# First attention of a two-layer encoder: q, k and v split by token and transposed by DMA, rope tables that carry the norm weights, O divided from PSUM

## The chip, the cores and the metric

The kernel runs on one core of a Trainium2 chip. The core has TensorE (PE, with its weight loads PEld), VectorE (DVE), ScalarE (ACT), GpSimd (POOL) and SyncE (SP), which here issues most of the DMAs. The metric is the device time of one execution in microseconds; the time of a kernel is the median of its runs. A profile shows one execution, with every instruction's start and duration.

## The reference

Two layers of an encoder trunk on one sequence of 1024 tokens of width 1024. Layer 0 mixes tokens by multi-head latent attention, layer 1 by dilated window attention, and each ends with a squared-ReLU MLP. The change is in layer 0's mixer:

```python
proj = h @ w_in
q_lat, kv_lat = proj[..., :384], proj[..., 384:640]
k_rope = rope(proj[..., 640:], pos)
q = (rms_norm(q_lat, g_qa) @ w_qb).reshape(B, S, 16, 96)
kv = (rms_norm(kv_lat, g_kva) @ w_kvb).reshape(B, S, 16, 128)
q = concat([q[..., :64], rope(q[..., 64:], pos)])
k = concat([kv[..., :64], broadcast(k_rope)])
v = kv[..., 64:]
q, k = rms_norm(q, g_q), rms_norm(k, g_k)
o = dense_attention(q, k, v, 96 ** -0.5)      # softmax over all 1024 keys, 16 heads
y = o.reshape(B, S, 1024) @ w_o
```

Products that need more than 16 bits of precision are made from two f16 parts, a high and a low one: high x high, high x low, low x high.

## The kernel before, in words

**Heads stage** (in `mla`, pool `psB`, lines 882 to 953). For each half of the heads (`hf`, 8 heads) and each tile of 128 tokens (`t`): TensorE makes q (two batches of 4 heads, 384 columns) and kv (two of 512 columns) in four PSUM banks (`mm3`, lines 522 to 524). ACT squares them (L905, L907), DVE sums the squares (L909, L910) and `rstd` makes 1/rms. DVE multiplies q and k by it into the f32 tile `st` (L921, L924), ACT copies v (L920), POOL writes the rotary part of k (L926) and rotates q (`rope`, L599 to L604, six instructions a batch). SP stores `st`, 256 f32 a token and head, to the DRAM tensor `qkv` (L933). The norm weights of q and k are multiplied together into one column `gq`. In the second half, the loads, preparations and maxima of heads 0 and 1 stand between the steps. This stage is put in order by the language's scheduler, except where an instruction is pinned.

**Preparation of a head** (`prep_load`, `prep`). Two loads bring the head's rows of `qkv` back (L813). TensorE turns q and k, four f32 transposes at a time (L826). ACT writes the high half from PSUM, scaled by `gq` or 64 (L156), and DVE the low half (L158). v is split the same way from SBUF into a tile with a column of ones (L161). A 97th row of k is a constant, that of q is minus the row's maximum, so that the score matmul subtracts it.

**Maxima** (`rowmax`, `rowstore`). For each of 8 tiles of queries and each half of the keys one matmul of high parts (L859) and a DVE reduction (L861). Then a small reduction (L867), a transpose to a row (L868), an ACT copy (L870), and two DMA steps through DRAM put it into q's row 96 (L871, L872).

**Attention** (`attention`). 128 slots, n = 8 x head + key tile. In a slot PE does two score banks of three 512-column matmuls (L1139 to L1141), then the AV products of slot n - 3 (L1178 to L1182): p is stationary, v moves, and for each of 8 query tiles the columns hold p_high x (v_high, 1, v_low) and p_low x (v_high, 1). ACT makes the exponentials (L1150), ACT or DVE the high half (L1154, L1152), POOL, or DVE in one slot of 8, the low half (L1161). At a head's end ACT and DVE copy the two AV banks out (`evict`), DVE takes reciprocals (L1201), and POOL adds the two v parts and divides (L1204 to L1208). For each pair of heads O is turned (L1217) and split (`spread`). The lists `todo`, `mid`, `late` and `end` say what else a slot does and where; `pin_from` keeps every engine in the order in which the code emits. Every fourth slot `ada_step` loads 512 KB of weights and adds 1024 columns on DVE (L261). PSUM has three score banks, two AV banks and three banks ("t") for everything else: maxima, transposes, sums.

After attention follow the output projection, layer 0's MLP and layer 1.

Of the kernel before, what the change touches and what calls it, by code (L numbers as in the profile page):

```python
# [20 lines left out]
P = 128  # L21
# [20 lines left out]
class K:  # L42
# [83 lines left out]
    def rstd(self, ms, n, name, up=False):  # L126

        nc = self.nc
        y = self.sm(name + "y", n)
# [72 lines left out]
    def const_loads(self):  # L202
# [16 lines left out]
        for r, src in ((5, "mla_g_q"), (6, "mla_g_k")):  # L219
            nc.gpsimd.dma_start(out=self.rows2[r : r + 1, 0:QK], in_=a[src])  # L220

# [383 lines left out]

    def w_in(self, d):
# [14 lines left out]
    def mla(self, xs, ada0, xs1, mods, tail):  # L621
# [177 lines left out]
        if half:  # L799
            most = self.M("most", [P, 16])  # L800
            nc.gpsimd.memset(most, 0.0)
            lnp = self.M("lnp", [P, 1])
            nc.gpsimd.memset(lnp, 10.0 * math.log(2.0))
        qkv = self.DR([H, S, 256], "qkv")
# [3 lines left out]
        ld, rd = (self.DR([H, S], x) for x in ("lrow", "rrow"))  # L808
# [6 lines left out]
        def prep(h, part, pt):  # L815
# [13 lines left out]
            if half:  # L829
                self.parts(hi, lo, pt[0:QK, :], gq if n == "q" else 64.0, check=False)  # L830
                if part < 2:
                    v4, ts = hd["v"][:, 0:1032].rearrange("p (t e) -> p t e", e=129), slice(4 * i, 4 * i + 4)
                    self.parts(v4[:, ts, 0:64], v4[:, ts, 65:129], hd["raw"][i][:, :, 192:256])
                    if i == 1:
                        nc.gpsimd.memset(v4[:, :, 64:65], 1.0)
                return
# [25 lines left out]

        def rowstore(h, ps):

            if half:
                nm = self.sm("nm", 8)
                nc.vector.tensor_reduce(nm, maxes.pop(h).rearrange("p (j b) -> p j b", b=2), op=ALU.max, axis=AX.X, negate=True)  # L867
                nc.tensor.transpose(ps[0:8, 0:P], nm, self.ident)  # L868
                mr = self.T("mr", (8, P), F16)
                nc.scalar.activation(mr, ps[0:8, 0:P], AF.Copy, scale=1.0 / 128)  # L870
                nc.sync.dma_start(out=md[h].rearrange("(t p) -> t p", p=P), in_=mr)  # L871
                nc.sync.dma_start(out=heads[h]["qh"][QK : QK + 1, :], in_=md[h : h + 1, :])  # L872
                return
# [8 lines left out]
        with tc.tile_pool(name="psB", bufs=8, space=PSUM, reuse_waits="tile") as psp:  # L882
            B = lambda name: psp.tile([P, 512], F32, tag="b", name=self.nm(name))
            raw = None
            for hf in range(2):
                w = hw[hf]
                for t in range(NT):
# [12 lines left out]
                    st = [self.G("st", (P, 4, 256), F32) for b in range(2)]  # L900
# [12 lines left out]
                    r = self.rstd(ms, 16, "hr", half)  # L913
                    if half:
                        y4 = self.sm("y4", 16)
                        nc.gpsimd.tensor_tensor(y4, r, r, op=ALU.mult)
                        nc.gpsimd.tensor_tensor(y4, y4, y4, op=ALU.mult)
                        nc.gpsimd.tensor_tensor(most, most, y4, op=ALU.add)
                    for b in range(2):
                        nc.scalar.activation(st[b][:, :, 192:256], kv4[b][:, :, 64:128], AF.Copy, scale=2.0 ** -7 if half else 1.0)  # L920
# [3 lines left out]
                        nc.vector.tensor_tensor(st[b][:, :, 96:160], kv4[b][:, :, 0:64],  # L924
                                                rk.broadcast_to([P, 4, 64]), op=ALU.mult)
                        nc.gpsimd.tensor_tensor(st[b][:, :, 160:192], rk.broadcast_to([P, 4, 32]),  # L926
                                                kr[:, t : t + 1, :].broadcast_to([P, 4, 32]), op=ALU.mult)
                    for b in range(2):
                        qr = st[b][:, :, 64:96]
                        self.rope(nc.gpsimd, qr, qr, *(self.cs[k][:, t : t + 1, :].broadcast_to([P, 4, 16])  # L930
                                                       for k in ("cos", "sin")), 4, "qr")
                        h0 = hf * 8 + b * 4
                        nc.sync.dma_start(out=qkv[h0 : h0 + 4, ts, :].rearrange("h t e -> t h e"), in_=st[b])  # L933
                    if hf == 0:
# [6 lines left out]
                        raw = heads_load(1, t) if t < 5 else None  # L941
                    else:
# [13 lines left out]
        if half:  # L956
            self.nseen += 1
            s_ = self.seen[:, self.nseen - 1 : self.nseen]
            nc.vector.tensor_reduce(s_, most, op=ALU.add, axis=AX.X)
            nc.vector.tensor_scalar(s_, s_, 2.0 ** 41, None, op0=ALU.mult)  # L960
            return self.attention(heads, gq, lnp, prep_load, prep, rowmax, rowstore, tail), None
# [151 lines left out]
    def attention(self, heads, gq, lnp, prep_load, prep, rowmax, rowstore, tail):  # L1113
# [5 lines left out]
        OP, U = {}, {}  # L1119
        with tc.tile_pool(name="psC", bufs=2, space=PSUM, reuse_waits="tile") as psp:  # L1120
# [3 lines left out]
            todo, mid, late, end = {}, {}, {}, {}  # L1124
# [21 lines left out]
            def weights(n, ps):  # L1146

                p, q = self.G("p", dt=F32), self.G("pp", (P, 2, 1024), F16)
                for b in range(2):
                    nc.scalar.activation(p[:, b * 512 : (b + 1) * 512], ps[b], AF.Exp, scale=1.0 / self.ss, bias=lnp)  # L1150
                if n % 8 in (0, 5):
                    nc.vector.tensor_copy(q[:, 0], p)  # L1152
                else:
                    nc.scalar.activation(q[:, 0], p, AF.Copy)  # L1154
                ps_p[n] = p, q

            def low(n):

                p, q = ps_p[n]
                eng = nc.vector if n % 8 == 3 or n > N - 4 else nc.gpsimd  # L1160
# [3 lines left out]
            def av(n):  # L1164
# [4 lines left out]
                v = heads[h]["v"][:, kt * 129 : kt * 129 + 129]  # L1169
                q = ps_p.pop(n)  # L1170
                mm = nc.tensor.matmul
                for b, ps in enumerate(ps_u[h]):
                    for i in range(4):
                        c = slice((4 * b + i) * P, (4 * b + i + 1) * P)
                        o = ps[:, 129 * i : 129 * i + (129 if i < 3 else 65)]
                        st = kt == 0 and i == 0
                        if i < 3:
                            mm(o, q[:, 0, c], v, start=st, stop=False)  # L1178
                        else:
                            mm(o, q[:, 0, c], v[:, 0:65], start=False, stop=False)  # L1180
# [1599 lines left out]
```

## Time and profile before

| what | value |
|---|---|
| median of 3 runs | 3082.59 us (3081.91 to 3087.77) |
| the profiled execution | 3090.18 us, its span 3088.3 us |
| busy: PE, DVE, ACT, POOL | 93%, 76%, 54%, 30% of the span |
| mean DMA rate | 161 GB/s |

The busy shares are of the whole span, in which stages with different limits follow each other. A row of a group of instructions gives line, engine, operation, the tiles out and in, shapes, count, then busy us and the mean ns of one, then the idle time of the engine ahead of it and what ended that. A row of the timeline gives start and duration in us.

### The profile page before, as it was taken

How to read it: one execution, taken by the hardware profiler on the slowest of the kernel's cores; microseconds unless marked ns; L12 is line 12 of the kernel's file. 1: busy time of each engine (PE TensorE's matmuls, PEld its weight loads, DVE VectorE, ACT ScalarE, POOL GpSimd, SP SyncE). 2: the span in 40 equal slices, each digit the busy share in tenths (PEclk: the TensorE clock that was granted, in tenths of full speed). 3: DMA queues.
4: the chain of work that ended last, by engine and by line, in shares of the span. 5: the costliest groups of instructions: out<-in, count | busy, mean ns of one | idle time of the engine just before them, and what ended most of it. 6: DMA issues, size and time to landing. Idle time of an engine off the chain costs nothing. (4 is left out here: it accounts for less than half of the span.)

```text
span 3088.3 us, 53769 instructions
## 1 busy us (share of the span) xinstructions
PE 2876.5 (93%) x19636; PEld 1712.4 (55%) x19636; DVE 2340.4 (76%) x5049; ACT 1666.9 (54%) x3443; POOL 933.3 (30%) x1521
## 2 busy tenths in 40 slices
PE   5998888889999999999999999997998999999998
PEld 4744555554444444444448878886876444444443
DVE  4688878865898895679867777776887589779665
ACT  3546777672545543443127787776665265545431
POOL 6376777660021100000113343443554002110010
PEclk7999999999999999999999999999998999999999
DMA  5253221141565579755734766675656556447653
GB/s 201 73 195 113 76 83 60 66 144 68 196 239 177 211 239 300 216 195 182 249 117 120 162 136 141 144 166 113 137 124 153 148 191 214 161 152 275 231 196 96
DMA packets 485053, 498.73 MB, mean 161 GB/s; under 512 B 191781, under 2 KB 373330, under 8 KB 484778
## 3 DMA queue, kind: packets, MB, share of 16 engines
q1 hardware_dynamic: 449162, 396.56, 44.0%
q0 software_dynamic: 25184, 87.12, 7.6%
q10 hardware_dynamic: 10432, 11.54, 1.5%
q8 instruction: 155, 2.54, 0.3%
q14 instruction: 120, 0.98, 0.1%
HBM read 329.90 MB, written 125.12 MB: 147 GB/s over the span
## 5 line engine op out<-in xcount | busy, mean ns | idle before, releaser
L522 PE MATMUL psm<-hf,wf 128*128 128x512 f16 x896 | 340.6, 380 | 6.3 <-ACT wf L156 6.3
L523 PE MATMUL psm<-d,d 128*128 128x512 f16 x896 | 340.5, 380 | 4.7 <-DVE d L161 4.7
L524 PE MATMUL psm<-hf,wf 128*128 128x512 f16 x896 | 334.9, 380 | 7.6 <-DVE wf L161 7.6
L524 PE MATMUL psm<-d,d 128*128 128x512 f16 x896 | 340.5, 380 | 0.0
L523 PE MATMUL psm<-hf,wf 128*128 128x512 f16 x896 | 340.3, 380 | 0.0
L522 PE MATMUL psm<-d,d 128*128 128x512 f16 x896 | 334.7, 380 | 0.3 <-ACT d L156 0.3
L522 PE MATMUL psproj<-wqk,hTp 128*128 128x256 f16 x1024 | 284.4, 278 | 0.0
L523 PE MATMUL psproj<-wqk,hTp 128*128 128x256 f16 x1024 | 283.6, 277 | 0.0
L524 PE MATMUL psproj<-wqk,hTp 128*128 128x256 f16 x1024 | 283.2, 277 | 0.0
L1161 POOL TENSOR_TENSOR pp<-p,pp 128x1024 f16<-128x1024 f32 x109 | 244.0, 2247 | 103.2 <-ACT pp L1154 81.4
L156 ACT ACTIVATE d<-ufr 128x1024 f16<-128x1024 f32 x112 | 117.8, 1052 | 205.3 <-PE psm L524 168.2
L161 DVE SCALAR_TENSOR_TENSOR d<-ufr,d 128x1024 f16<-128x1024 f32 x112 | 136.5, 1219 | 77.9 <-ACT d L156 77.7
L861 DVE TENSOR_REDUCE mx<-pmx 128x1 f32<-128x512 f32 x256 | 163.0, 678 | 23.5 <-PE pmx L859 23.4
L1150 ACT ACTIVATE p<-pss,lnp 128x512 f32<-128x512 f32 x256 | 163.0, 679 | 22.3 <-PE pss L1141 21.2
L2259 ACT ACTIVATE pd<-pd,dnb 128x192 f32<-128x192 f32 (+2 forms) x384 | 167.3, 437 | 4.2 <-POOL y L2187 2.2
L524 PEld LDWEIGHTS <-wf 128*128 128x128 f16 x896 | 87.8, 98 | 118.3 <-DVE wf L161 14.0
L522 PEld LDWEIGHTS <-wf 128*128 128x128 f16 x896 | 87.7, 98 | 114.5 <-ACT wf L156 12.2
L524 PEld LDWEIGHTS <-d 128*128 128x128 f16 x896 | 87.7, 98 | 110.6 <-issue 5.7
L522 PEld LDWEIGHTS <-d 128*128 128x128 f16 x896 | 87.9, 98 | 106.3 <-issue 1.9
L523 PEld LDWEIGHTS <-d 128*128 128x128 f16 x896 | 87.8, 98 | 106.0 <-issue 1.7
L2297 POOL TENSOR_TENSOR ph<-pd,ph 128x512 f16<-128x512 f32 (+1 forms) x121 | 113.2, 942 | 108.2 <-ACT ph L2296 108.0
L523 PEld LDWEIGHTS <-wf 128*128 128x128 f16 x896 | 87.8, 98 | 104.5 <-issue 1.0
(442 smaller groups left out, 8229.3 us busy)
## 6 DMA issues: line engine op xcount, KB each, us to landing
ufr<-uf SPq DMA_DIRECT2D x112, 512.0 KB
adaw<-in_ada_w SPq DMA_DIRECT2D x96, 512.0 KB
w2r<-in_mlp_w SPq DMA_DIRECT2D x96, 512.0 KB
w1r<-in_mlp_w SPq DMA_DIRECT2D x64, 512.0 KB
wqkr<-in_dil_w_in SPq DMA_DIRECT2D x96, 256.0 KB
wvr<-in_dil_w_in SPq DMA_DIRECT2D x34, 512.0 KB
qkv<-st SPq DMA_DIRECT2D x32, 512.0 KB
hraw<-qkv SPq DMA_DIRECT2D x32, 512.0 KB
```

Of the source, the lines that this page charges most:

```text
L156: nc.scalar.activation(hi, src, AF.Copy, scale=scale)
L161: return nc.vector.scalar_tensor_tensor(lo, src, scale, hi, op0=ALU.mult, op1=ALU.subtract, accum_out=self.seen[:, self.nseen - 1 : self.n ...
L522: mm(out, lh, rh, start=first, stop=False)
L523: mm(out, lh, rl, start=False, stop=False)
L524: mm(out, ll, rh, start=False, stop=last)
L861: nc.vector.tensor_reduce(maxes[h][:, 2 * j + b : 2 * j + b + 1], ps, op=ALU.max, axis=AX.X)
L1150: nc.scalar.activation(p[:, b * 512 : (b + 1) * 512], ps[b], AF.Exp, scale=1.0 / self.ss, bias=lnp)
L1161: eng.tensor_tensor(q[:, 1], p, q[:, 0], op=ALU.subtract)
L2259: nc.scalar.activation(p[:, e, lo:hi], p[:, e, lo:hi], AF.Exp, scale=1.0 / self.ss, bias=nb[:, e : e + 1], accum_out=stat[:, g, t, 1, 2 * ...
L2297: (nc.gpsimd if i or u["g"] == 2 else nc.vector).tensor_tensor(lo, p, hi, op=ALU.subtract)
```

## The change

**In the heads stage** q, k and v are split into f16 halves as they leave PSUM or `st`, and `qkv` becomes f16 with 512 columns for a token and head: q high, k high (192), q low, k low (192), v low, v high. The weights of both norms come as rows (two loads at the start), and `gain_tables` multiplies them once into the rope tables and into a table for q's first 64 columns. The rope of q takes four POOL instructions a batch in place of six. A running sum that guarded the range goes: 1/rms is kept for all steps and checked at the end.

```python
def rope_q(self, x, t):
    u, w = (... tile([P, 4, 32], F32) ...)
    c, s = (k[:, t : t + 1, :].broadcast_to([P, 4, 32]) for k in (self.cg, self.sg))
    eng.tensor_tensor(u, x, c, op=ALU.mult)
    eng.tensor_tensor(w[:, :, 0:16], x[:, :, 16:32], s[:, :, 0:16], op=ALU.mult)
    eng.tensor_tensor(w[:, :, 16:32], x[:, :, 0:16], s[:, :, 16:32], op=ALU.mult)
    eng.tensor_tensor(x, u, w, op=ALU.add)
```
```diff
-                    nc.gpsimd.tensor_tensor(y4, r, r, op=ALU.mult)
...
+                    for b in range(2):
+                        self.parts(s16[b][:, :, 448:512], s16[b][:, :, 384:448], kv4[b][:, :, 64:128], 2.0 ** -7)
...
-                    nc.scalar.activation(st[b][:, :, 192:256], kv4[b][:, :, 64:128], AF.Copy, scale=2.0 ** -7 if half else 1.0)
...
+                    self.rope_q(st[b][:, :, 64:96], t)
+                    nc.vector.tensor_tensor(st[b][:, :, 0:64], st[b][:, :, 0:64],
+                                            gt[:, 0:64].unsqueeze(1).broadcast_to([P, 4, 64]), op=ALU.mult)
+                    nc.scalar.activation(s16[b][:, :, 0:192], st[b], AF.Copy)
+                    nc.gpsimd.tensor_tensor(s16[b][:, :, 192:384], st[b], s16[b][:, :, 0:192], op=ALU.subtract)
+                    nc.sync.dma_start(out=qkv[h0 : h0 + 4, ts, :].rearrange("h t e -> t h e"), in_=s16[b])
```

**A head's preparation** is now DMAs alone: four transposes from `qkv`, a constant row, and v.

```diff
+        def fetch(h):
+            hd = heads[h] = {}
+            for n, o in (("q", 0), ("k", 96)):
+                hd[n] = x = self.G(n, (P, 2, 1024), F16)
+                hd[n + "h"], hd[n + "l"] = x[0 : QK + 1, 0], x[0 : QK + 1, 1]
+                for i in range(2):
+                    nc.sync.dma_start_transpose(out=x[:, i : i + 1, :], in_=qkv[h][:, o + 192 * i : o + 192 * i + P])
+        def ones(h):
+            nc.sync.dma_start(out=hd["kh"][QK : QK + 1, :], in_=self.onerow)
+            v = hd["v"] = self.G("hv", (P, 8, 129), F16)
+            nc.gpsimd.memset(v[:, :, 128:129], 1.0)
+            nc.sync.dma_start(out=v[:, :, 0:128], in_=qkv[h][:, 384:512].rearrange("(t p) e -> p t e", p=P))
```

**In attention** `rowstore` becomes `topmost` (reduction), `turn` (transpose) and `mrow` (ACT and the two DMA steps), each in a slot of its own. ACT casts every high half, POOL makes every low half but the last three. The AV products add all three parts into the same 65 columns, and DVE divides from PSUM.

```diff
-                        if i < 3:
-                            mm(o, q[:, 0, c], v, start=st, stop=False)
...
+                        o = ps[:, 65 * i : 65 * i + 65]
+                        mm(o, q[:, 0, c], v[:, 64:129], start=kt == 0 and i == 0, stop=False)
+                        mm(o[:, 0:64], q[:, 0, c], v[:, 0:64], start=False, stop=False)
+                        mm(o, q[:, 1, c], v[:, 64:129], start=False, stop=kt == 7 and i == 3)
...
             def finish(h):
+                for b, ps in enumerate(ps_u.pop(h)):
+                    x = ps[:, 0:260].rearrange("p (i e) -> p i e", e=65)
+                    nc.vector.reciprocal(r[:, 4 * b : 4 * b + 4], ps[:, 64:260:65])
+                    nc.vector.tensor_tensor(OP[h // 2][:, 4 * b : 4 * b + 4, h % 2 * 64 : h % 2 * 64 + 64], x[:, :, 0:64],
+                                            r[:, 4 * b : 4 * b + 4].unsqueeze(2).broadcast_to([P, 4, 64]), op=ALU.mult)
...
             for h in range(1, H):
                 if h > 2:
-                    put(8 * h - 16, prep_load, h)
+                    put(8 * h - 18, fetch, h)
+                    put(8 * h - 14, ones, h)
-                for j, m in enumerate((10, 9, 9, 8, 7, 7, 6, 5)):
+                for j in range(8):
...
+                        put(j // 2 if h == 1 else 8 * h - 12 + j, lambda h, j, b: rowmax(h, j, b, PT("pmx")), h, j, b, to=mid)
-                put(8 * h - 4, lambda h: rowstore(h, PT("pmt")), h, to=late)
+                put(8 * h - 5, topmost, h, to=late)
+                put(8 * h - 4, lambda h: turn(h, PT("pmt")), h, to=late)
+                put(8 * h - 3, mrow, h, to=soon)
             for h in range(H):
-                put(8 * h + 7 + LAG, evict, h, to=late)
-                put(8 * h + 8 + LAG, finish, h, to=end)
+                put(8 * h + 7 + LAG, finish, h, to=late)
                 if h % 2:
                     for th in range(2):
-                        put(8 * h + 11 + LAG + th, spread, h // 2, th, to=late)
+                        put(8 * h + 9 + LAG + th, spread, h // 2, th, to=late)
+                        put(8 * h + 10 + LAG + th, keep, h // 2, th, to=soon)
```

`keep` is the split that `spread` did. The list `soon` runs ahead of a slot's exponentials. In the second half of the heads stage head 0 is fetched at t = 0 and head 1 at t = 1, head 0's maxima come at t = 2 to 5, `topmost` at 6, `turn` and `mrow` at 7; before, the maxima came at t = 4 to 6 and their row at 6.

More of the change, by code (lines that the diff above doesn't have):

```diff
@@ L220, in const_loads @@
             nc.gpsimd.dma_start(out=self.rows2[r : r + 1, 0:QK], in_=a[src])
+        if self.half:
+            self.gains = self.G("gains", (P, 2, QK), F32)
+            for i, src in enumerate(("mla_g_q", "mla_g_k")):
+                nc.gpsimd.dma_start(out=self.gains[:, i], in_=a[src].broadcast_to([P, QK]))
     def conditioning(self):
@@ L861, in rowmax, with topmost, turn, mrow @@
             nc.vector.tensor_reduce(maxes[h][:, 2 * j + b : 2 * j + b + 1], ps, op=ALU.max, axis=AX.X)
-        def rowstore(h, ps):
[L865 to L873, printed above, removed]
+        def topmost(h):
+            nm = heads[h]["nm"] = self.sm("nm", 8)
+            nc.vector.tensor_reduce(nm, maxes.pop(h).rearrange("p (j b) -> p j b", b=2), op=ALU.max, axis=AX.X, negate=True)
+        def turn(h, ps):
+            heads[h]["pm"] = ps
+            nc.tensor.transpose(ps[0:8, 0:P], heads[h].pop("nm"), self.ident)
+        def mrow(h):
+            mr = self.T("mr", (8, P), F16)
+            nc.scalar.activation(mr, heads[h].pop("pm")[0:8, 0:P], AF.Identity, scale=1.0 / 128, bias=lnp[0:8])
+            nc.sync.dma_start(out=md[h].rearrange("(t p) -> t p", p=P), in_=mr)
+            nc.sync.dma_start(out=heads[h]["qh"][QK : QK + 1, :], in_=md[h : h + 1, :])
+        def rowstore(h, ps):
             nm = self.sm("nm", 8)
@@ L899, in mla @@
                     kv4 = [x.rearrange("p (h e) -> p h e", e=128) for x in pkv]
[L900 removed]
+                    st = [self.G("st", (P, 4, 192 if half else 256), F32) for b in range(2)]
+                    s16 = [self.G("s16", (P, 4, 512), F16) for b in range(2)] if half else None
                     sq = self.G("sq", (P, 8 * QK), F32)
@@ L941, in mla @@
                         raw = heads_load(1, t) if t < 5 else None
+                    elif half:
+                        for f, x in {0: ((fetch, 0),), 1: ((ones, 0), (fetch, 1)), 2: ((ones, 1),), 6: ((fetch, 2), (topmost, 0)),
+                                     7: ((ones, 2), (turn, 0), (mrow, 0))}.get(t, ()):
+                            f(x, *((B("pmt"),) if f is turn else ()))
+                        if 2 <= t < 6:
+                            for j in (2 * t - 4, 2 * t - 3):
+                                [rowmax(0, j, b, B("pmx")) for b in range(2)]
                     else:
@@ L958, in mla @@
             s_ = self.seen[:, self.nseen - 1 : self.nseen]
-            nc.vector.tensor_reduce(s_, most, op=ALU.add, axis=AX.X)
+            for _ in range(2):
+                nc.gpsimd.tensor_tensor(rall, rall, rall, op=ALU.mult)
+            nc.vector.tensor_reduce(s_, rall, op=ALU.add, axis=AX.X)
             nc.vector.tensor_scalar(s_, s_, 2.0 ** 41, None, op0=ALU.mult)
-            return self.attention(heads, gq, lnp, prep_load, prep, rowmax, rowstore, tail), None
+            return self.attention(heads, fetch, ones, rowmax, topmost, turn, mrow, tail), None
         O = [[[None] * 4 for _ in range(2)] for _ in range(2)]
@@ L1111, in mla, with attention @@
         return O, oTd
-    def attention(self, heads, gq, lnp, prep_load, prep, rowmax, rowstore, tail):
+    def attention(self, heads, fetch, ones, rowmax, topmost, turn, mrow, tail):
         nc, tc = self.nc, self.tc
```

108 lines of the change are left out of this document (49 added, 59 removed).

## The prediction

> **What bounds the kernel now.** I read the page first, then the table of windows over the three stretches that the diff can touch, then the waits inside attention, then the order of instructions on TensorE. The profiled execution took 3090.18 us around this span; the median of the runs is 3082.59, so I work in differences on the profile and take them off the median.
>
> ```profile
> span 3088.3 us, 53769 instructions
> ```
>
> Windows: start and end, length, busy us (instructions) of PE, PEld, DVE, ACT, POOL, then granted clock, DMA share and GB/s.
>
> ```profile
> 137.00:243.00 106.00, 95.86 (x505) 50.30 (x504) 85.45 (x199) 52.31 (x145) 73.56 (x256) 0.97 0.58 190
> 243.00:679.00 436.00, 377.77 (x3643) 232.85 (x3642) 347.43 (x525) 317.40 (x487) 313.66 (x230) 0.96 0.25 84
> ```
>
> The first row is the heads stage (16 steps: 8 token tiles for each half of the heads), the second attention: 436 us for 16 heads of 8 slots, 27.25 us a head. The diff leaves what follows alone. In attention no engine is full: a head has 21.7 us of DVE, 19.8 of ACT, 19.6 of POOL. PE's busy time counts each matmul to its modelled end, so its real need has to come from start to start:
>
> ```profile
> 399.97 0.62 PE L826 MATMUL pqk<-ident,hraw 128*96 128x128 f32 x4
> 400.43 0.38 PE L1139 MATMUL pss<-q,k 97*128 97x512 f16 x1
> ...
> 402.25 0.22 PE L1178 MATMUL pav<-hv,pp 128*128 128x129 f16 x1
> 402.30 0.19 PE L1182 MATMUL pav<-hv,pp 128*128 128x65 f16 x1
> 402.33 0.20 PE L1180 MATMUL pav<-hv,pp 128*128 128x65 f16 x1
> 402.36 0.20 PE L1181 MATMUL pav<-hv,pp 128*128 128x64 f16 x1
> 402.40 0.19 PE L1182 MATMUL pav<-hv,pp 128*128 128x65 f16 x1
> 402.43 0.38 PE L859 MATMUL pmx<-k,q 96*128 96x512 f16 x1
> 402.65 0.22 PE L1178 MATMUL pav<-hv,pp 128*128 128x129 f16 x1
> ```
>
> A 512-column matmul holds PE 0.22 us (402.43 to 402.65), a 129-column one 0.05 to 0.06, a 65-column one 0.03 to 0.04 even four in a row, four f32 transposes 0.46. A head now needs 48 score matmuls (10.6), 16 for the maxima (3.5), 16 blocks of nine for AV at 0.36 (5.8), 16 transposes of q and k (1.8), and 0.6 for turning O and the maxima: 22.3 us of the 27.25. So TensorE is the longest engine by a little, and 5 us a head are waits. PE's largest ones between 260 and 650 us (total, times, longest):
>
> ```profile
> PE pmx L859 <- DVE mx L861: 16.2, 18, 1.4
> ...
> PE psot L1217 <- DVE q L158: 10.9, 6, 1.8
> ...
> PE pmt L868 <- DVE nm L867: 10.4, 13, 1.1
> ```
>
> All three end with DVE. They make 37.5 us in 390, 2.6 a head; the other 2.4 are the clock (0.96 granted) and gaps to which the view gives no releaser.
>
> **The change, part by part.** *Attention.* The rows of each engine in 260 to 650 us:
>
> ```profile
> L861 DVE TENSOR_REDUCE mx<-pmx 128x1 f32<-128x512 f32 x227 | 144.8, 678 | 19.7 <-PE pmx L859 19.6
> L261 DVE SCALAR_TENSOR_TENSOR adacc<-adaw,cond,adacc 128x1024 f32<-128x1024 f32 x21 | 44.7, 2130 | 0.0
> L1152 DVE CAST pp<-p 128x1024 f16<-128x1024 f32 x28 | 29.2, 1044 | 11.1 <-ACT p L1150 11.1
> L161 DVE SCALAR_TENSOR_TENSOR hv<-hraw,hv 128x256 f16<-128x256 f32 x27 | 21.4, 793 | 0.0
> L158 DVE SCALAR_TENSOR_TENSOR q<-pqk,gq,q 96x512 f16<-96x512 f32 x28 | 20.8, 741 | 33.5 <-ACT q L156 33.5
> ...
> L158 DVE SCALAR_TENSOR_TENSOR oT<-psot,oT 128x512 f16<-128x512 f32 x12 | 8.3, 691 | 4.5 <-ACT oT L156 4.5
> ...
> L1201 DVE RECIPROCAL ll<-ot 128x4 f32<-128x4 f32 x28 | 3.2, 152 | 0.0
> ```
> ```profile
> L1150 ACT ACTIVATE p<-pss,lnp 128x512 f32<-128x512 f32 x228 | 145.1, 679 | 15.2 <-PE pss L1141 14.1
> L1154 ACT ACTIVATE pp<-p 128x1024 f16<-128x1024 f32 x85 | 89.8, 1057 | 5.1
> ...
> L156 ACT ACTIVATE oT<-psot 128x512 f16<-128x512 f32 x12 | 7.2, 597 | 33.9 <-PE psot L1217 33.9
> L870 ACT ACTIVATE mr<-pmt 8x128 f16<-8x128 f32 x15 | 4.0, 266 | 22.4 <-PE pmt L868 22.4
> ```
> ```profile
> L1161 POOL TENSOR_TENSOR pp<-p,pp 128x1024 f16<-128x1024 f32 x99 | 221.0, 2240 | 95.7 <-ACT pp L1154 77.4 <-DVE pp L1152 16.5 <-DVE mod L313 0.6
> ```
> ```profile
> L924 DVE TENSOR_TENSOR st<-pkv,hry 128x256 f32<-128x256 f32 x32 | 13.2, 413 | 0.0
> ```
>
> The last row is of the heads stage and prices the new division of O from PSUM: the same shape, twice a head. After the change a head needs:
> - PE: 10.6 + 3.5, AV as 192 short matmuls at 0.03 (5.8, at most 6.4), 0.6: 20.5 us. The 1.8 of transposes goes; splitting the wide AV matmul costs nothing, since columns set the pitch.
> - ACT: 16 x 0.679 + 8 x 1.057 + 0.60 + 0.27 = 20.2. It loses the q, k, v halves and an eviction, and takes two casts from DVE: no gain.
> - DVE: 16 x 0.678 + two sums of the ada weights at 2.13 + 2 x (0.15 + 0.41) + 0.69 = 16.9, against 21.7.
> - POOL: 8 x 2.24 = 17.9, against 19.6.
>
> So PE and ACT share a floor of 20.5. The waits on top: `topmost` a slot ahead of `turn` ends the wait of `pmt` (0.7 a head); O no longer passes through POOL and `keep` is a slot behind `spread`, so of the 0.8 behind `psot` I leave 0.2; the maxima, two in every slot and with DVE lighter, keep 0.6 of their 1.1. The 2.4 without a releaser I scale with DVE's load, to 1.7. One wait is new. `finish` stands in DVE's order behind the ada sum of slot 8h+1 and frees the two AV banks that slot 8h+3 starts with, and the whole of PE is queued behind that matmul. What the sum takes there:
>
> ```profile
> L261 DVE SCALAR_TENSOR_TENSOR adacc<-adaw,cond,adacc x21: 1270/1274/3103, 292.0 to 626.4; 128x1024 f32<-128x1024 f32 x21
> ```
>
> 1.27 or 3.10 us, the long ones beside a running POOL instruction. DVE's work from the first maximum of slot 8h+1 (0.9 us into it) is four maxima 2.7, the sum 2.1 to 3.1, `finish` 1.1: 5.9 to 6.9, while PE is there after 2 x 2.56 + 1.5 - 0.9 = 5.7. Late by 0.2 to 1.2; I take 0.8. Together 0.2 + 0.6 + 1.7 + 0.8 = 3.3, so 23.8 us a head, and 16 x (27.25 - 23.8) = **55 us saved** (floor 20.5: 108; at 25.5 a head: 28).
>
> *DMA.* Four transposes a head, each 1024 x 128, take the place of two loads, and stand in SP's queue six slots (about 14 us) ahead of the head's first maxima. The row for a DMA transpose here is of the second layer; behind it the two steps of the maxima's row, which stay:
>
> ```profile
> L2298 SPq DMA_TRANSPOSE pT<-ph x93: 1232/1609/5410, 1640.8 to 2377.3; - x93
> ```
> ```profile
> 340.94 0.28 SPq L871 DMA_DIRECT2D mrow<-mr  x1
> 342.14 0.21 SPq L872 DMA_DIRECT2D q<-mrow  x1
> ```
>
> Four take 6.4 us of SP at the median and 21.6 at the longest, both within a head: hidden, 0. `mrow` moves a slot later; three slots (7.6 us) are left for ACT and two DMA steps of about 1.2 each, so it is hidden too.
>
> *Heads stage.* Added for each of 16 steps, two batches each: the v split, the norm table on q, the f16 copies. Rows of 136 to 250 us:
>
> ```profile
> L158 DVE SCALAR_TENSOR_TENSOR latT<-pslt,latT 128x256 f16<-128x256 f32 x2 | 0.8, 412 | 0.0
> ```
> ```profile
> L926 POOL TENSOR_TENSOR st<-hry,kr 128x128 f32<-128x128 f32 x32 | 12.1, 399 | 0.0
> L602 POOL TENSOR_TENSOR qrw<-st,sin 128x64 f32<-128x64 f32 x32 | 11.6, 362 | 0.0
> ```
>
> DVE: v 32 x 0.41 = 13.2 and the norm table 32 x 0.41 = 13.2, less the 8 us that heads 0 and 1 took there (eight rows like L158 q, four like L161 hv at 0.5 to 0.8): 85.5 + 18.4 = 104. The table has two SBUF inputs like the ada sum, which waited 1.8 us for POOL; at one rope instruction (0.36) of waiting each, 11.5 more: 116. POOL: the rope goes from 12 instructions at 0.36 to four at 0.40 and four at 0.36, less 1.3; the low halves are 0.75 of L1161, 2 x 1.68; +2.1 x 16: 107. PE stays under 96. ACT adds 1.6 a step and has 52 of 106. So DVE, now 81% busy, becomes the bound: 106 to 116, +10. Bounds: 0, if steps overlap well, and +40, if each table multiplication waits for a low half (1.2 more). The hand-over: head 0's maxima are turned after the last step's matmuls, and score 0 waits for ACT and two DMA steps, 2.7 to 8 us where it waited for q's low half before: +5. `gain_tables` and the two loads are some ten POOL instructions of that size, and lie under PE's projections: 0, or +3 if not. At the end of attention O skips POOL's four steps: -2.
>
> Sum: -55 + 10 + 5 - 2 = **-42**: 3048 for the profiled execution, 3041 for the median.
>
> **The rivals.**
> *Waits gone* (faster): PE and ACT in step, no late `finish`; 21.5 to 22 a head, -84 to -92, with +10 at hand-over: about 3004. For it: DVE falls to 0.8 of a slot. Against: three score banks only, and the locked sums.
> *Heads stage eats it*: attention at 25 a head (-36) and the stage +30 by waits of the table for POOL: 3077, no gain to speak of.
> *Transposes pace the heads* (slower): source rows are 256 B out of 1024 in DRAM, and the row above reads SBUF. With 2 us a head for SP's other issues, one transpose over (23.8 - 2) / 4 = 5.4 us makes SP the bound, and over 6.1 (26.4 a head) all is lost. At 8 us, half over the longest seen, a head takes 34: +108 in attention, +15 before it, 3206. Against: median 1.6 in 93.
> By the Trainium skill, "VectorE: DVE Perf Modes", section on the three transpose paths, a 128 x 128 transpose takes 1309 ns by DMA and 390 on TensorE, and the advice is TensorE where PSUM will do. Eight blocks would be 10.5 us, 42 a head, an estimate of some 3330 us. Row L2298 speaks against it: its transposes have up to 16 blocks and most issue within 1.6 us, though it times the issue.
> *It doesn't free what bounds*: ACT's 20.2 is no less than now, so if ACT set the slot nothing would move. L1150 waits 14.1 us for PE, so I count this within the second rival.
>
> **How the numbers follow.** Forecast (22.5 to 25 a head) 0.50, waits gone 0.20, heads stage eats it 0.20, transposes 0.05, other handovers on the slow side 0.05. A measurement can tell 0.2%, 6 us. Faster: 0.50 + 0.20 + half of the third = 0.80; same 0.08; slower 0.12. The range goes from the second case (3003) to just past the third (3080); the forecast's own is 3020 to 3065.
>
> **What would show it.** Right: maxima of neighbouring heads about 24 us apart; no L826; `pmt` without a DVE wait; a wait of the first AV matmul for DVE's division; DVE over 95% in the heads stage and score 0 later than 243 us. Wrong: PE waiting for DMA at L859 (transposes), ACT without idle time in front of its exponentials (the fourth), or heads at 27 us.

## The result, and the profile after

The changed kernel took 3027.88 us (median of four runs, 3027.27 to 3034.2) beside 3082.25 (3078.36 to 3087.77) of the kernel before on the same chip: a ratio of 0.9827, interval 0.9807 to 0.9847. The forecast was 3041, range 3003 to 3080: sign and total came out, but the terms behind them did not. Two misses of opposite sign hide each other in the sum, and that the total came so near is luck.

The profiled execution took 3027.27 us against 3090.18, 63 us less where the medians say 54, as the profile of before lies 8 us above its median. To see where the 63 us lie, I take the first and the last start of four groups of matmuls: q of the heads stage (`pq`), scores (`pss`), the maxima's transpose (`pmt`) and the output projection (`psy`). A row has the least, median and largest duration in ns, then the first and the last start in us. Before:

```profile
L522 PE MATMUL pq<-wh,latT x96: 322/326/528, 124.7 to 237.8; 128*128 128x384 f16 x96
L868 PE MATMUL pmt<-ident,nm x15: 272/273/274, 262.7 to 644.6; 128*8 128x128 f32 x15
L1139 PE MATMUL pss<-q,k x256: 375/380/635, 243.2 to 673.1; 97*128 97x512 f16 x128
L522 PE MATMUL psy<-wo,oT x256: 376/379/634, 683.1 to 2482.1; 128*128 128x512 f16 x128
```

And after:

```profile
L526 PE MATMUL pq<-wh,latT x96: 322/326/528, 127.4 to 265.4; 128*128 128x384 f16 x96
L910 PE MATMUL pmt<-ident,nm x15: 271/271/271, 295.2 to 592.5; 128*8 128x128 f32 x15
L1208 PE MATMUL pss<-q,k x256: 376/380/634, 278.8 to 617.8; 97*128 97x512 f16 x128
L526 PE MATMUL psy<-wo,oT x256: 376/379/631, 625.0 to 2419.6; 128*128 128x512 f16 x128
```

The spans end at 3088.3 and 3025.5. So the work ahead of the stage takes 2.7 us more (124.7 to 127.4), the stretch from the first q to score 0 grows from 118.5 to 151.4 (+33), attention from score 0 to the first `psy` shrinks from 439.9 to 346.2 (-94), and the rest goes from 2405.2 to 2400.5 (-5, untouched by the diff). Below I call these two stretches the heads stretch and attention. A head takes (644.6 - 262.7) / 14 = 27.3 us before and (592.5 - 295.2) / 14 = 21.2 after. The same two stretches in the table of windows, columns as before:

```profile
137.00:279.00 142.00, 101.65 (x490) 50.21 (x488) 120.82 (x287) 68.72 (x166) 111.23 (x189) 0.87 0.53 149
279.00:623.00 344.00, 332.85 (x4175) 204.75 (x4173) 241.56 (x372) 292.18 (x420) 282.48 (x147) 0.99 0.49 114
```

Attention is now full of PE (333 of 344 us, clock 0.99). The heads stage has 120.8 us of DVE in 142 and less of every other engine: no engine is full in it from end to end. All waits of PE between 295 and 610 us:

```profile
PE pmx L898 <- DVE mx L900: 6.7, 6, 1.1
PE pss L1208 <- ACT p L1219: 1.6, 2, 0.8
```

The wait for `psot` (10.9 us before) and the one for `pmt` (10.4) are gone, that for the maxima fell from 16.2, and no AV matmul waits for DVE's division.

### The profile page after: what moved, and what is told of

Read it like the earlier page. It is cut to its first block, busy times and chain, and to the rows that moved or that the text cites. A ratio compares the mean times of both kernels' runs of the same rounds, so it can differ in the third digit from the quotient of the medians.

```text
span 3025.5 us, 54508 instructions
## 1 busy us (share of the span) xinstructions
PE 2834.8 (94%) x20148; PEld 1682.3 (56%) x20148; DVE 2275.6 (75%) x4985; ACT 1656.4 (55%) x3395; POOL 944.5 (31%) x1372
## 5 line engine op out<-in xcount | busy, mean ns | idle before, releaser
L526 PE MATMUL psm<-hf,wf 128*128 128x512 f16 x896 | 340.7, 380 | 6.3 <-ACT wf L156 6.3
L1227 POOL TENSOR_TENSOR pp<-p,pp 128x1024 f16<-128x1024 f32 x125 | 275.5, 2210 | 56.2 <-ACT pp L1220 39.0
L900 DVE TENSOR_REDUCE mx<-pmx 128x1 f32<-128x512 f32 x256 | 173.2, 687 | 78.8 <-PE pmx L898 77.5
L1219 ACT ACTIVATE p<-pss 128x512 f32<-128x512 f32 x256 | 150.2, 591 | 47.4 <-PE pss L1210 46.0
L526 PEld LDWEIGHTS <-wf 128*128 128x128 f16 x896 | 87.9, 98 | 114.6 <-ACT wf L156 12.2
```

The lines of the kernel that those rows point to most:

```text
L526: mm(out, lh, rh, start=first, stop=False)
L900: nc.vector.tensor_reduce(maxes[h][:, 2 * j + b : 2 * j + b + 1], ps, op=ALU.max, axis=AX.X)
L1227: eng.tensor_tensor(q[:, 1], p, q[:, 0], op=ALU.subtract)
```

## The experiments

A single run can't tell 5 us in the whole: the untouched rest spreads from 2399.7 to 2410.6 us over the profiles below. So kernels with one run are judged by the stretches, and the three with four runs by their ratio to the kernel before, run on the same chip. The six profiles in which the heads stage is the same, but for one DMA in one of them, put its stretch at 150.8 to 151.7 us and its first eight steps at 65.1 to 66.1, so 1 us there tells nothing.

### Attention: what made the head shorter

**DVE's load given back, all else kept.** The later maximum of each pair is taken twice, 8 x 0.69 = 5.5 us a head, which brings DVE back to what it had:

```diff
             nc.vector.tensor_reduce(maxes[h][:, 2 * j + b : 2 * j + b + 1], ps, op=ALU.max, axis=AX.X)
+            if half and h > 0 and b == 1:
+                nc.vector.tensor_reduce(self.sm("dup", 1), ps, op=ALU.max, axis=AX.X)
```

> Takes every second maximum of heads 1 to 15 twice on DVE (8 more reductions of 0.69 us a head, the extra result unused): DVE's work per head goes from 15.3 back to 20.8 us, about what it was before (21.7), with order, hand-offs and everything else as in the changed kernel. Theory A, attention was freed by DVE's lighter load: heads at 24 to 27 us in place of 21.2, PE waiting for DVE at the maxima's matmul again. Rival B, it was freed by the order (two maxima a slot, the maxima's row in three slots, O's split a slot later): heads at 21 to 22.5 us.

Measured: 3089.86 us, attention 403.8, a head 25.2. PE's largest waits from 295 to 640 us, and the window:

```profile
PE pav L1244 <- DVE O L1258: 28.9, 12, 2.5
PE pmx L898 <- DVE mx L900: 8.0, 11, 1.1
```
```profile
295.00:640.00 345.00, 307.99 (x3608) 184.92 (x3606) 301.06 (x439) 249.63 (x356) 242.71 (x123) 0.94 0.41 91
```

This is the wait that the prediction feared: the first AV matmul of a head behind `finish`, 2.4 us each time. It stands there once DVE has 301 of 345 us, and is absent in the changed kernel (218 of 305). So in the new order DVE's load alone is worth 4.0 of the 6 us that a head gained. It comes back as another wait than those of the kernel before (`pmx`, `psot`, `pmt`); what the same load would cost or spare in the old order was not tried.

**The order of the maxima as before.** Two of six slots hold two tiles of queries, where the changed kernel has one in each of eight, and the row comes in one go:

```diff
-                for j in range(8):
+                for j, m in enumerate((10, 9, 9, 8, 7, 7, 6, 5)):
...
-                put(8 * h - 5, topmost, h, to=late)
-                put(8 * h - 4, lambda h: turn(h, PT("pmt")), h, to=late)
-                put(8 * h - 3, mrow, h, to=soon)
+                for f in (topmost, lambda h: turn(h, PT("pmt")), mrow):
+                    put(8 * h - 4, f, h, to=late)
```

> The order of a head's maxima as before: unevenly over six slots (two, four or none a slot), the small reduction, the transpose and the row all in slot 8h - 4. Work as in the changed kernel. Theory A, DVE's load alone freed attention (giving the load back took heads from 21.2 to 25.2 us): heads at 21.2 to 21.8 us, since DVE at 73% keeps up with the bunches. Rival B, the order has a share of its own: 22.5 us or more, with PE waits at the maxima and at the transpose, as before (0.7 to 1.8 us a head).

Measured: 3047.61 us, attention 365.5, 22.6 us a head: the order is worth 1.3 us a head, some 20 in all. The waits that were expected at the maxima and their transpose hardly show (2.2 us and none); again it is the division that comes late (same stretch):

```profile
PE pav L1242 <- DVE O L1256: 15.9, 12, 1.4
```

**O evicted, added and divided by POOL as before.** `evict`, the wide AV products, the old `finish` and the split of O right behind `spread`, two slots later, come back; the rest stays changed. Of the edit:

```diff
-                put(8 * h + 7 + LAG, finish, h, to=late)
+                put(8 * h + 7 + LAG, evict, h, to=late)
+                put(8 * h + 8 + LAG, finish, h, to=end)
...
```

> O goes its old way: wide AV matmuls of 129 columns, both AV banks copied out by ACT and DVE, the two v parts added and divided by POOL, turned and split two slots later. ACT gains 0.55 us a head, POOL 4.3 (to 22.0). Theory A: DVE's load is hardly changed, so heads stay near POOL's 22 us (22 to 22.5, +12 to +20 us in all). Rival B, O's way through POOL made the waits: heads alternate as before, the odd ones 3 us or more longer, PE waits at the transposes of O: 24 us or more on average, +45 us.

Measured: 3041.39 us, attention 359.2, 21.8 us a head: 0.6 lost. POOL has 319 of 345 us in the window:

```profile
295.00:640.00 345.00, 326.71 (x3343) 196.95 (x3340) 246.39 (x345) 283.93 (x421) 318.68 (x230) 0.99 0.51 111
```

That is a little under the 22 of the first theory. PE's waits there are small and end with ACT (`pss`, 7.1 us), POOL (7.4) and DVE (`pav`, 3.4). So of DVE's load (4.0 us a head), the order (1.3) and the path of O (0.6) the load is the large one. Each was put back alone; how they act together was not tried.

**The exponential with a bias tile again.** The change has one more edit, which the text ahead of the prediction does not show: the exponential lost its bias column `lnp`. The experiment gives it the tile `eps` as bias.

```diff
-                    nc.scalar.activation(p[:, b * 512 : (b + 1) * 512], ps[b], AF.Exp, scale=1.0 / self.ss)
+                    nc.scalar.activation(p[:, b * 512 : (b + 1) * 512], ps[b], AF.Exp, scale=1.0 / self.ss, bias=self.eps)
```

> The exponential gets a bias tile again (a constant of 1e-6 a partition, which changes nothing that can be seen), as before the change. It took 679 ns with the bias tile and 591 without. If the bias operand is what costs, the L1219 row goes back to 670 to 685 ns and ACT's need to 20.3 us a head, still under PE's 20.5: heads at 21.3 to 21.9, +2 to +10 us in all. If the shorter time has another cause (less contention, fewer waits), the row stays near 591 ns and nothing moves.

> The bias tile on the exponential again, now with repeated times. In its first look ScalarE's exponential was 89 ns longer and the kernel 4.4 us faster. Theory L (TensorE sets the attention's pace and a slower exponential only moves the other engines against each other): 3022 to 3026 us, -2 to -5 beside the 3027.9 of the changed kernel. Rival N (the first look was a chance): 3027 to 3029.

The first run gave 3022.83 us (attention 341.1), where 2 to 10 us more than the changed kernel had been expected; the four later runs gave 3021.83 (3019.02 to 3023.47), ratio 0.9781 (0.9765 to 0.9798), an interval wholly below that of the changed kernel. The rows of the exponential and of the ada sum between 295 and 600 us, changed kernel first:

```profile
L1219 ACT ACTIVATE p<-pss 128x512 f32<-128x512 f32 x229 | 135.2, 591 | 38.4 <-PE pss L1210 37.0
...
L265 DVE SCALAR_TENSOR_TENSOR adacc<-adaw,cond,adacc 128x1024 f32<-128x1024 f32 x21 | 38.5, 1833 | 0.0
```
```profile
L1219 ACT ACTIVATE p<-pss,eps 128x512 f32<-128x512 f32 x233 | 156.7, 679 | 15.2 <-PE pss L1210 7.0
...
L265 DVE SCALAR_TENSOR_TENSOR adacc<-adaw,cond,adacc 128x1024 f32<-128x1024 f32 x21 | 28.2, 1343 | 0.0
```

ACT's instruction is 88 ns longer and the head 0.4 us shorter. ACT had 38 us of idle time ahead of its exponentials, so PE loses nothing. What gets better is the ada sum: the longest of the 21 takes 1.39 us, where 6 took 3.19 in the changed kernel. The waits for the maxima (6.7 us) vanish. That the shifted phase of ACT brings this about is argued; that a slower ACT costs nothing here is shown, by the pace of 20.7 to 20.8 us a head in all four profiles with the bias tile.

### Heads stretch: what made it longer

The growth of 33 us by steps (starts of each step's first `pq`): the first eight steps went from 52.7 to 65.9 us (+13.2), the next ones up to the start of the last from 56.5 to 69.8 (+13.3), and from the last step to score 0 from 9.3 to 15.8 (+6.5). The first part, 137 to 178 us before and 137 to 193 after:

```profile
137.00:178.00 41.00, 40.20 (x220) 21.26 (x219) 34.75 (x83) 23.98 (x66) 32.59 (x107) 1.00 0.61 195
```
```profile
137.00:193.00 56.00, 45.92 (x231) 23.60 (x229) 52.45 (x122) 32.16 (x75) 42.05 (x72) 0.91 0.42 128
```

PE was the full engine (40.2 of 41); now DVE is the fullest (52.5 of 56), and PE waits for it, `pq` for the banks that DVE's L969 reads:

```profile
PE pq L526 <- DVE st L969: 9.2, 3, 4.3
```

Two of DVE's rows before (136 to 250 us), then, after (137 to 279 us), the new row of the norm table and the same two, which grew:

```profile
L911 DVE TENSOR_SCALAR hms<-hms,krss 128x8 f32<-128x8 f32 x16 | 5.6, 347 | 0.3
L134 DVE SCALAR_TENSOR_TENSOR hrt<-hms,hry 128x16 f32<-128x16 f32 x16 | 3.3, 207 | 7.1 <-ACT hry L133 7.0
```

```profile
L984 DVE TENSOR_TENSOR st<-st,gt 128x256 f32<-128x256 f32 x32 | 18.1, 578 | 0.0
...
L959 DVE TENSOR_SCALAR hms<-hms,krss 128x8 f32<-128x8 f32 x16 | 9.8, 612 | 0.0
L134 DVE SCALAR_TENSOR_TENSOR hrt<-hms,rall 128x16 f32<-128x16 f32 x16 | 6.3, 395 | 6.3 <-ACT rall L133 6.2
```

**The norm table left out; the low halves on ACT; both.**

```diff
-                            nc.vector.tensor_tensor(st[b][:, :, 0:64], st[b][:, :, 0:64],
-                                                    gt[:, 0:64].unsqueeze(1).broadcast_to([P, 4, 64]), op=ALU.mult)
```
```diff
-                            nc.gpsimd.tensor_tensor(s16[b][:, :, 192:384], st[b], s16[b][:, :, 0:192], op=ALU.subtract)
+                            nc.scalar.activation(s16[b][:, :, 192:384], st[b], AF.Copy, scale=0.0)
```

> Leaves out the multiplication of q's first 64 columns by the norm weights (32 DVE instructions of 582 ns, 18.6 us, in a heads stage of 142 us, 137 to 279 us in the profile after). Theory C, DVE sets the heads stage (121 of its 142 us are busy): score 0 comes 15 to 22 us earlier, near 260 us. Rival D, POOL's low halves set it (48 us of instructions in 125): no more than 4 us earlier. Rival E, the hand-over of head 0 (maxima, DMA) sets it: no change. Attention unchanged in all, near 346 us from the first score matmul to the first of the output projection.

> Leaves out the low halves of q and k: ACT writes zeros in their place (32 instructions of some 0.84 us on ACT, which is busy 69 of the stage's 142 us), POOL loses 32 of 1.68 us. Theory C: only the time that DVE's instructions wait for POOL goes, some 15 to 20 us (the L959 row at 637 ns against 347 before, L134 and L135 at 410 and 376 against 207 and 195, the weight halves at 2.0 to 2.5 us against 1.1 to 1.3), so score 0 near 261 us. Rival D, the low halves themselves are the chain: 30 us or more, score 0 back at 245 to 250 us.

> The changed kernel without the multiplication of q by the norm table (the output has no norm weights on q's first 64 columns) and with the low halves of q and k made by ScalarE as zeros instead of GpSimd's difference (their low parts are left out). Alone, the first shortened the stretch from the first q matmul to score 0 by 5.0 us (151.4 to 146.4) and the second by 3.0. Theory C (a step of the heads stage is a chain DVE, GpSimd, ScalarE, GpSimd that comes back to DVE, and what one engine gives up the next one takes): both together shorten it by 15 us or more, to 136 or less. Rival P (the stretch is set elsewhere: by the step's own eviction, squares and rope, or by heads 0 and 1 between the steps): the two add up, about -8, to 143.

Measured: heads stretch 146.4, 148.4 and 142.3 us (whole 3020.59, 3028.68, 3025.16), against 151.4. The first two were each expected to bring 15 us or more, by the theory that DVE sets the stage; they brought 5.0 and 3.0, so it fell. The two gains add up (9.1 together), as the rival had it; the theory of a chain in which one engine takes over what another gives up, with 15 or more for both, fell too. The first eight steps gained next to nothing (64.6, 66.7 and 65.7 us); the gains lie in the steps after them. What the second one shows beside that is who lengthened DVE's small instructions. Without POOL's 1.68 us low halves the same rows read:

```profile
L984 DVE TENSOR_TENSOR st<-st,gt 128x256 f32<-128x256 f32 x32 | 16.6, 535 | 0.0
...
L959 DVE TENSOR_SCALAR hms<-hms,krss 128x8 f32<-128x8 f32 x16 | 3.6, 227 | 0.0
L134 DVE SCALAR_TENSOR_TENSOR hrt<-hms,rall 128x16 f32<-128x16 f32 x16 | 2.8, 175 | 21.7 <-ACT rall L133 21.6
```

With both edits DVE has only 38.9 us in the same 56, and yet the first eight steps take 65.7:

```profile
137.00:193.00 56.00, 45.09 (x233) 23.45 (x232) 38.86 (x113) 41.50 (x93) 22.38 (x64) 0.94 0.46 146
```

ACT's largest waits there name a candidate for what holds them, the second half's weights, whose loads stand in SP's queue behind the stores (total, times, longest):

```profile
ACT wh L156 <- DMA wqr<-in_mla_w_qb: 4.9, 2, 2.6
...
ACT wh L156 <- DMA wkvr<-in_mla_w_kvb: 2.5, 1, 2.5
```

**Those loads ahead of the stores.** All five pairs are issued at the start of the stage.

```diff
-            raw = None
+            raw, ahead = None, [heads_load(1, i) for i in range(5)] if half else []
...
-                        raw = heads_load(1, t) if t < 5 else None
+                        raw = (ahead[t] if half else heads_load(1, t)) if t < 5 else None
```

> Heads stage: the five weight loads of the second half of the heads are issued ahead of the loop and no longer stand in SP's queue behind the stores of q, k and v. Neither leaving out the norm table nor the low halves shortened the first half of the stage (65.8 us for 8 steps, 64.6 and 66.7 without them, 52.7 before). Theory F, these loads, late behind stores that wait for POOL, hold up ACT, and DVE and PE behind it: the first half takes 56 to 60 us, score 0 comes 5 to 10 us earlier. Rival C, DVE with its waits for POOL: 64 to 66 us, score 0 within 2 us.

Measured: 3033.64 us, heads stretch 149.4 (2.0 less), first eight steps 67.9: the theory of the loads fell. DVE has only 48.6 of the same 56 us there, so with the loads early the eight steps are held by neither the loads nor a full DVE; their first step alone takes 14.8 us where it took 12.1. Early loads and a light DVE together were not tried.

**ACT's order.** In the changed kernel ACT does squares, v, then the f16 copies of the step before, and only then this step's 1/rms, so that this waits for POOL's rope of the step before. Here the copies are tied behind the next step's 1/rms, and low halves and store behind its rope (with the bias tile as well, so the kernel with the bias tile is what to compare with). Of the edit:

```diff
                     r = self.rstd(ms, 16, "hr", half, rall[:, i : i + 16] if half else None)
+                    for f in late[0]:
+                        self.held(f)
...
```

> With the bias tile as before. In the heads stage the f16 copies of a step's q and k (ScalarE) are tied behind the logarithm and exponential of the next step's 1/rms, and the low halves and the store behind the next step's rope on GpSimd; nothing is added or left out. In the changed kernel ScalarE's order is squares, v, copies of the step before, then the 1/rms of this step, so the 1/rms waits for the rope of the step before. Theory Q (that order is the loop that sets the step: 1/rms behind copies behind rope behind 1/rms): the first 8 steps shrink from 65.8 us to 58 or less, the stretch from the first q matmul to score 0 from 151.7 to 140 or less, and the whole from 3021.8 to about 3010. Rival D (VectorE's own 52 of 56 us hold the step): the order frees little, the first 8 steps stay above 63 and the stretch above 147.

Measured: 3024.38 us, ratio 0.9784 (0.9765 to 0.9804), no better than 0.9781; heads stretch 149.3 against 151.7, first eight steps 65.9. The theory of the order fell. What the heads stretch gains, attention loses: it takes 346.9 us where the bias tile alone gave 340.7, although its heads keep the pace of 20.8 us; the maxima of head 1 are turned 20.3 us behind score 0 in place of 14.2. The window has DVE at 51.6 of 56, as the rival said, and in the next row ACT waits for DVE:

```profile
137.00:193.00 56.00, 45.36 (x230) 23.30 (x229) 51.55 (x123) 32.78 (x79) 42.83 (x75) 0.94 0.38 116
```
```profile
ACT hrl L132 <- DVE hms L959: 12.1, 6, 5.1
```

So no edit shortened the first eight steps by more than 1.3 us: not 13.6 us less of DVE's work, not early loads, not another order on ACT. That they have two limits at almost one pace, DVE's instructions and a step's way through ACT, POOL and the loads, so that taking one away brings the other out, fits these runs but is argued: none took both away, and what sets these +13.2 us stays open.

**Head 0's maxima in the steps.** In the second half one step takes 21.3 us (207.85 to 229.17) where the longest before took 11.6: most of the +13.3. It is the one after which head 0's first four maxima come. PE, then ACT and DVE around it (start, duration, idle ahead and its releaser):

```profile
207.85 0.34 PE L526 MATMUL pq<-wh,latT 128*128 128x384 f16 x1 [2.56 <-ACT sqk L955]
...
214.84 0.38 PE L528 MATMUL pkv<-wh,latT 128*128 128x512 f16 x1
221.35 1.87 PE L898 MATMUL pmx<-k,q 96*128 96x512 f16 x4 [6.13 <-DVE st L969]
229.17 0.48 PE L526 MATMUL pq<-wh,latT 128*128 128x384 f16 x1 [5.96 <-DVE mx L900]
```
```profile
213.96 0.38 ACT L955 ACTIVATE sqk<-pkv 128x256 f32<-128x256 f32 x1 [5.38 <-PE pkv L528]
215.25 0.39 ACT L955 ACTIVATE sqk<-pkv 128x256 f32<-128x256 f32 x1 [0.91 <-PE pkv L528]
215.53 1.56 ACT L986 ACTIVATE s<-st 128x768 f16<-128x768 f32 x2
217.00 0.86 ACT L953 ACTIVATE sq<-pq 128x384 f32<-128x384 f32 x2
```
```profile
217.90 0.95 DVE L957 TENSOR_REDUCE hms<-sq 128x8 f32<-128x768 f32 x1 [6.84 <-ACT sq L953]
...
220.69 0.56 DVE L969 TENSOR_TENSOR st<-pq,rall 128x384 f32<-128x384 f32 x1
```

Read it from PE's second wait back. The maxima use the same eight PSUM banks as the steps, four of them at once, so they wait until DVE has read a step's q (L969, done at 221.25). DVE sat idle for 6.8 us because ACT's squares of q came late: in ACT's order kv's squares, which wait for the step's last matmul, and the two copies of the step before stand ahead of them. Then the next step's q waits for the maxima's banks, whose reductions stand in DVE's order behind the next 1/rms, up to 229.1. Each engine waits for the next and none is full: of the 21.3 us PE has 9.2, DVE 12.2, ACT 8.1 and POOL 17.0. Head 0's transposes, which stand in SP's queue behind the first half's last store, were issued by 220.3:

```profile
218.53 1.78 SPq L847 DMA_TRANSPOSE k<-qkv  x1
```

PE's wait ends with DVE, so they are no more than a close second there. With ACT's order freed (the kernel above) this step takes 17.2 us, and where the maxima come a step later (the last kernel below) theirs takes 17.1. Without POOL's low halves (ACT writes zeros in their place) it takes 16.5, and 15.7 without the norm table as well: POOL's work is part of this step's length, which the reading of PE's waits alone does not show.

At the end of the stage SP's queue delays head 0's row: ACT has it ready at 270.0, and its first DMA goes out at 274.19, behind four transposes of head 2.

```profile
269.64 0.36 ACT L915 ACTIVATE mr<-pmt,lnp 8x128 f16<-8x128 f32 x1 [0.55 <-PE pmt L910]
```
```profile
271.46 2.63 SPq L847 DMA_TRANSPOSE k<-qkv  x2
274.19 0.43 SPq L916 DMA_DIRECT2D mrow<-mr  x1
```

**The row ahead of head 2's transposes.**

```diff
-                        for f, x in {..., 6: ((fetch, 2), (topmost, 0)),
-                                     7: ((ones, 2), (turn, 0), (mrow, 0))}.get(t, ()):
+                        for f, x in {..., 6: ((topmost, 0), (turn, 0), (mrow, 0), (fetch, 2)), 7: ((ones, 2),)}.get(t, ()):
```

> Hand-over: head 0's maxima are turned and their row sent at t = 6, ahead of head 2's four transposes in SP's queue, in place of t = 7 and behind them (the row's DMA was issued at 274.2 us, 4.2 after ACT had it ready at 270.0). Theory E, the hand-over is 7 us of the stage's growth: score 0 comes 5 to 9 us earlier (270 to 274 us in place of 278.8), right behind the last step's matmuls. Rival: score 0 then waits for something else, head 1 or DVE's backlog, and gains under 2 us.

Measured: 3027.89 us; the row goes out at 263.0, eleven us earlier, but score 0 only from 278.8 to 277.1, the heads stretch from 151.4 to 150.5, which is inside the spread, as the rival had it. Score 0 still stands 9.4 us behind the last PE instruction, and starts while DVE makes its last reads of the stage's PSUM banks (L969 and L973, 275.6 to 277.3). The view names no releaser for it (`issue`):

```profile
PE pss L1208 <- issue: 9.4, 1, 9.4
```

So the row is not what holds score 0 alone. The row and DVE's last reads end together: in the changed kernel the wait of score 0 ends with DVE (`st`, L984, 9.2 us), in the kernel with the bias tile, whose heads stage is the same, with the row's second DMA (`q<-mrow`, 9.6 us). That the last step's banks are the other limit (the attention's PSUM pools begin where the stage's end) fits the times but was not tried by itself.

**All together**: loads ahead, row ahead, head 0's maxima at steps 3 to 5 in place of 2 to 5, bias tile.

> Four edits on the changed kernel: the second half's weight loads ahead of the stores in the sync queue, head 0's row ahead of head 1's last fetch, head 0's maxima at steps 3 to 5 instead of 2 to 5, the bias tile on the exponential. Alone, the first brought score 0 forward by 3.6 us, the second by 1.7, the last the end of attention by 5. If they add: score 0 at 272 us or before and the whole 3016 to 3021 us. If the end of the heads stage is set by the last step alone (rival): score 0 at 275 to 277 and the whole 3020 to 3025 us.

Measured: 3031.41 us, ratio 0.9812 (0.9796 to 0.9829), heads stretch 153.0, score 0 at 280.2. That is worse than both the sum and the rival had it. The small gains don't add; the first eight steps even took 69.0 us, and score 0 now waits for a DMA, the constant row that SP issues late:

```profile
PE pss L1208 <- DMA k<-onerow: 10.5, 1, 10.5
```

No version is better than the changed kernel with the bias tile.

## Why the prediction was right in the total, and wrong in its terms

- *Floor of a head, 20.5 us of PE*: right. A head takes 21.2 us in the changed kernel and 20.8 with the bias tile. ACT, DVE and POOL were forecast at 20.2, 16.9 and 17.9 a head and have 18.0, 15.2 and 17.6 (the busy times of the row below by 21.2 / 305):

```profile
295.00:600.00 305.00, 298.34 (x3794) 185.68 (x3792) 217.94 (x338) 258.84 (x375) 253.29 (x128) 1.00 0.49 105
```

  ACT's miss is the exponential at 0.591 instead of 0.679 (16 x 0.088 = 1.4 a head), an edit I had overlooked; most of the rest is overlap, as ACT's rows add up to 272 us where the window, counting each moment once, has 258.8; DVE's is the ada sum, 1.5 a head at 1.83 instead of two at 2.13.
- *Waits on top, 3.3 us a head*: this is the mis-sized term; it is 0.7. Maxima 0.6 forecast, 6.7 us in 315 or 0.45 a head measured. `psot` 0.2, measured none. The late `finish` 0.8, measured none: it was worked out with DVE at 5.9 to 6.9 us from the first maximum on, and the ada sum is mostly short. The 1.7 "without a releaser" was scaled with DVE's load; about 0.3 is left. These gaps do not shrink in proportion to DVE's load but all but vanish, and with the load given back some 2.0 a head return (25.2 less the floor of 20.5 and 2.7 of waits in the view). The granted clock goes the same way, 0.96 before, 1.00 after, 0.94 with the load back, so how much of the gaps was the clock and how much waits for DVE stays open. That waits for DVE stand above the floor was right, and the run with DVE's load given back shows it: the late `finish` comes at 25.2 us a head. Attention saved 94 us, not 55, a little more than the rival "waits gone".
- *Transposes of the heads hidden at 0 in attention*: right, no wait of PE there ends with a DMA. By the Trainium skill, "VectorE: DVE Perf Modes", section on the three transpose paths, eight 128 x 128 blocks by DMA would be 10.5 us, 42 a head, an estimate from its 1309 ns a block. The measured head of 21.2 refutes that as a pace, with a median issue of 1.6 and 1.3 us:

```profile
L847 SPq DMA_TRANSPOSE q<-qkv x32: 1159/1599/2437, 212.6 to 554.5; - x32
L847 SPq DMA_TRANSPOSE k<-qkv x32: 1170/1297/2258, 216.4 to 557.2; - x32
```

- *Heads stage +10, hand-over +5*: wrong by size; +33, with +3 ahead of it, a little more than the rival "heads stage eats it". DVE's work came out near its size, 116 us forecast and 120.8 measured, in part by luck (next point but one). POOL's 107 left out that the running sum's three instructions a step go (L916 to L918, 10.3 us); it measured 111.2, the low halves at the 1.68 forecast and the rope longer than forecast (53.7 us for 48.6). The step that failed is the one from DVE's work to the time, that the stage would run at DVE's pace. In the first eight steps DVE is the fullest (52.5 of 56), but with 13.6 us of its work gone they take as long; in the second half DVE has 79% (68.4 of 86 us), and one step alone loses 10 us, in which engine waits for engine around head 0's maxima. I had priced each engine's work, and no chain through the orders of four engines and the eight banks.
- *Hand-over*: score 0 after the last step, +6.5 against +5. The path was half right: the row ends together with DVE's last reads, and sent eleven us earlier it shortened the stretch by no more than 0.9.
- *Ada sums and the new table wait for POOL*: the table was put at 0.41 + 0.36 and takes 0.58; unforeseen were the small instructions (L959 from 347 to 612 ns, L134 from 207 to 395). The first miss takes 6 us off DVE's sum, the second adds some 7 to it: that the sum fits is luck to that extent.
- *`gain_tables` 0 or +3*: the stage starts 2.7 us later in this profile, 1.0 to 2.7 in all the others with the same tables, so within the bounds, if it is they; that was not tried.
- *What would show it*: `pmt` without a DVE wait, no L826 and score 0 later than 243 us (278.8) came true; heads 24 us apart (21.2), an AV matmul waiting for the division (none) and DVE over 95% in the stage (85% over the whole, 94% in its first half) did not.

In sum: -94 +33 +3 -5 = -63 us measured, where -55 - 2 +10 +5 = -42 was forecast. The forecast had 37 us too little gain and 21 too little loss; with the 5 of the untouched rest that leaves the 21 by which it fell short.

## What to carry to other kernels

Waits that end with an engine at 80% of the slot need not scale with its load: here, with DVE at 72%, they went almost altogether, and the next floor was the time. Work that is moved out of a full loop into a stage ahead of it is not priced by that stage's busiest engine: follow one step through the order of each engine and see who stands in front of whom, and which banks must be read first. And where two limits may run at nearly one pace, taking either away shows little; look for the waits that come up in its place before calling it innocent, and take both away before calling them the cause.

## What the runs showed of the hardware

An activation of 128 x 512 from PSUM takes 591 ns without a bias tile and 679 with one (rows above). The Trainium skill, "ScalarE: Activation LUTs", section "What ACT_TABLE_LOAD costs", gives about 93 ns for each pointer operand; the runs agree with 88. And beside a running POOL instruction even DVE's instructions on 8 or 16 columns wait: L959 has 612 ns with POOL's low halves and 227 without, L134 395 and 175.

In the heads stage, where PE waits more than before, the granted clock is lower too. It fell from 1.00 and 0.95 (first and second part before, PE busy 40.2 of 41 and 55.7 of 65 us) to 0.91 and 0.85 (45.9 of 56 and 55.7 of 86); not in step with PE's load, as the run without the norm table has 0.96 with 45.2 of 56. In the long step above, after PE had been idle for 2.6 us, the 384-column matmuls go from a start every 0.17 us to one every 0.32, with a granted clock of 0.52 from 208.35 to 211.80:

```profile
208.02 0.33 PE L527 MATMUL pq<-wh,latT 128*128 128x384 f16 x1
208.19 0.33 PE L528 MATMUL pq<-wh,latT 128*128 128x384 f16 x1
...
209.51 0.52 PE L527 MATMUL pq<-wh,latT 128*128 128x384 f16 x1
209.83 0.52 PE L528 MATMUL pq<-wh,latT 128*128 128x384 f16 x1
```
